# Early routing of tile 0, twice the early experts, and gate products in pairs in a transformer kernel

## The chip, the cores and the metric

The kernel runs on one core of one Trainium2 chip. The metric is device time in microseconds, measured over whole executions. Besides, one execution was recorded by the hardware profiler.

## The reference

Two transformer blocks over 512 tokens of width 1024. The first one mixes (attention, gated convolution) and then runs a layer of product-key experts, which is what the change touches. Cut to that:

```python
q = (hf @ w_query).reshape(t, 8, 256)
s1 = einsum('thd,hnd->thn', q[..., :128], peer_keys1)   # 128 scores
s2 = einsum('thd,hnd->thn', q[..., 128:], peer_keys2)
v1, i1 = top_k(s1, 16); v2, i2 = top_k(s2, 16)
cand = (v1[..., :, None] + v2[..., None, :]).reshape(t, 8, 256)
sc, ci = top_k(cand, 16)
idx = take(i1, ci // 16) * 128 + take(i2, ci % 16)      # 16 of 16384 experts, per head
gates = softmax(sc)
a = gelu(einsum('td,thkd->thk', hx, peer_u[idx]))
out = einsum('thk,thkd->td', gates * a, peer_v[idx])
```

The second block (MLA, HGRN2, feed-forward layers) follows and is not touched.

## The kernel before

Everything is float32 in effect: a matrix product is three TensorE passes (mm3) over a rounded high part and the rest. wload fetches 512 KB of weights (raw, four buffers), ScalarE rounds them to wh, VectorE subtracts to get wl (line 189; five buffers each). So each 512 KB costs one ScalarE and one VectorE pass before TensorE can use it.

Tokens form four tiles of 128. For tile 0 the experts are gathered: each of 256 steps (gathered, lines 754, 761, 770) has GpSimd fetch one 512 KB set of rows by an index tile (ui for peer_u, vi for peer_v; tile row, four buffers) and VectorE multiply it into a sum. The other three tiles (384 tokens) use all 16384 experts densely: 128 slices of peer_u give activations (expert_in, 24 matmuls into psu, Gelu to ga), which are multiplied by a dense gate matrix G, split into wgh and wgl, and multiplied with peer_v into the sums y.

The layer has two stages. *Routing* (peer_route): 16 query chunks on TensorE, whose scores VectorE ranks by top16 (five instructions for 16 values of one row set); topk ranks one head of one tile: two lists of 128 scores, then 80 candidate sums (cand), then those. Tiles 0 to 2 are ranked as the chunks come, tile 3 after tile 0 is finished (ui and vi written, line 702). For tiles 1 to 3 gate matrices follow, by one-hot masks (o, oh, ol; lines 729 to 732) and matmuls pg, stored to G. Into this stage are put *early experts*: fill keeps two running sums of assumed VectorE and TensorE time, and whenever TensorE's is behind, early runs expert_in for the next slice and stores its Gelu to DRAM (AD, line 800). There are 56 of these; two of their first subtractions run on GpSimd. *Products* (peer): 32 groups of four experts, first the 72 that were not early, then the 56 that were, whose ga are loaded from AD (seven buffers). Each ga is multiplied by its part of G (line 852) and split on its own. Gather steps are spread over the groups by a cost of 16 for a group of the first kind and 1 for one of the second.

```python
cost = [16 if e0 >= NE else 1.0 for e0 in groups]
rate = (256 - given[0]) / (sum(cost[:ng - 3]))
```

A scheduler decides each engine's final order by what waits for what; each engine then runs its list strictly in order.

Of the kernel before, what the change touches and what calls it, by code (L numbers as in the profile page):

```python
# [10 lines left out]
F32 = mybir.dt.float32  # L11
F16 = mybir.dt.float16
F32R = mybir.dt.float32r
I32 = mybir.dt.int32
U32 = mybir.dt.uint32
AF = mybir.ActivationFunctionType
ALU = mybir.AluOpType
# [140 lines left out]
class _Kernel:  # L158
# [421 lines left out]
        return out  # L580


    def expert_in(self, e2, pool=False):

        wh, wl = self.wload(self.a["peer_u"][e2], pool)
        ps = self.psa.tile([128, 512], F32, tag="a", name="psu")
        for k in range(8):
            s = slice(k * 128, k * 128 + 128)
            h, l = self.xs2[k]
            self.mm3(ps[:, :384], (wh[:, s], wl[:, s]), (h[:, 128:], l[:, 128:]), k == 0, k == 7)  # L590
        return ps[:, :384]
# [11 lines left out]
    def peer_route(self, p, G, fill, step):  # L603
# [14 lines left out]
        I = [p.tile([128, 4, 8, 16], U32, name=f"i{h}") for h in range(2)]  # L618
        SC = p.tile([128, 4, 8, 16], F32, name="SC")
        CI = p.tile([128, 4, 8, 16], U32, name="CI")  # L620
        qT, scores = {}, []

        def consume(n, ps):
            if n % 2 == 0:
                qT["k"] = p.tile([128, 2, 128], F32, tag="keys", name="keys", bufs=2)
                nc.sync.dma_start(qT["k"].rearrange("p a b -> p (a b)"), a["keys"][:, n * 128:(n + 2) * 128])
            o = self.work.tile([128, 512], F32, tag="full", name="qT", bufs=2)
            nc.scalar.activation(o, ps, AF.Copy)
            pt = self.pst.tile([128, 512], F32, tag="t", name="ptsc")
            for t in range(4):  # L630
                nc.tensor.matmul(pt[:, t * 128:(t + 1) * 128], o[:, t * 128:(t + 1) * 128], qT["k"][:, n % 2, :])
            if n % 8 == 0:
                scores.append(p.tile([128, 8, 4, 128], F32, tag="gt", name="sc", bufs=2))
            sc = scores[-1][:, n % 8]
            nc.scalar.activation(sc.rearrange("p a b -> p (a b)"), pt, AF.Copy)
            fill(1.2, 6.2)
            if n % 2 == 0:
                return
            for t in range(3):
                topk(t, n // 2)  # L640

        def topk(t, h):
            V = [self.small.tile([128, 16], F32, tag=f"v{x}", name=f"v{x}", bufs=2) for x in range(2)]
            for x in range(2):
                self.top16(V[x], I[x][:, t, h, :], scores[h // 4][:, h % 4 * 2 + x, t, :])


            cand = p.tile([128, 80], F32, tag="cand", name="cand", bufs=2)
            for i0, ni, nj, at in ((0, 2, 16, 0), (2, 2, 8, 32), (4, 4, 4, 48), (8, 8, 2, 64)):
                nc.vector.tensor_tensor(cand[:, at:at + ni * nj].rearrange("p (i j) -> p i j", j=nj),  # L650
                                        V[0][:, i0:i0 + ni, None].to_broadcast([128, ni, nj]),
                                        V[1][:, None, 0:nj].to_broadcast([128, ni, nj]), ALU.add)
            self.top16(SC[:, t, h, :], CI[:, t, h, :], cand)
            fill(3.0, 0.0)

        self.gemm_fm(self.xs2, [a["w_query"][c] for c in range(16)], consume)
        for t in range(4):
            sc = SC[:, t]
            g = p.tile([128, 8, 16], F32, tag="g", name="g", bufs=2)
# [18 lines left out]
            for x in range(2):  # L678
                ai = ij[x]
                af = p.tile([128, 8, 16], F16, tag="af", name="af", bufs=2)  # L680
                nc.vector.tensor_copy(af, ai)
                e = p.tile([128, 8, 16], F32, tag=f"e{x}", name=f"e{x}", bufs=2)
                for hh in range(2):

                    hs = slice(hh * 4, hh * 4 + 4)
                    ib = p.tile([128, 4, 16, 16], F16, tag="ib", name="ib", bufs=1)
                    nc.scalar.activation(ib, I[x][:, t, hs, :, None].to_broadcast([128, 4, 16, 16]), AF.Copy)
                    eq = p.tile([128, 4, 16, 16], F16, tag="eq", name="eq", bufs=1)
                    nc.vector.tensor_tensor(eq, iotaj[:, None].to_broadcast([128, 4, 16, 16]),
                                            af[:, hs, None, :].to_broadcast([128, 4, 16, 16]), ALU.is_equal)  # L690
                    nc.vector.tensor_tensor(eq, eq, ib, ALU.mult)
                    for w in (8, 4, 2):
                        nc.vector.tensor_tensor(eq[:, :, 0:w], eq[:, :, 0:w], eq[:, :, w:2 * w], ALU.add)
                    nc.vector.tensor_tensor(e[:, hs], eq[:, :, 0], eq[:, :, 1], ALU.add)
                    fill(2.2, 0.0)
                es.append(e.rearrange("p h k -> p (h k)"))
            fill(1.5, 0.3)
            if t == 0:
                ef = p.tile([128, 128], F32, tag="ef", name="ef", bufs=1)
                for dst, hi, lo in ((self.ui, es[0], es[1]), (self.vi, es[1], es[0])):  # L700
                    nc.vector.scalar_tensor_tensor(ef, hi, 128.0, lo, ALU.mult, ALU.add)
                    nc.vector.tensor_copy(dst, ef)
                nc.vector.tensor_copy(self.g0, g.rearrange("p h k -> p (h k)"))
                for tt in range(3, 4):
                    for h in range(8):
                        topk(tt, h)
                        for _ in range(2):
                            step()
                continue
            pt = self.pst.tile([128, 512], F32, tag="t", name="ptr")  # L710
            for n, src in enumerate((es[0], es[1], g.rearrange("p h k -> p (h k)"))):
# [8 lines left out]
            for c in range(4):  # L720
                gt = p.tile([128, 128, 32], F32, tag="gt", name="gt", bufs=2)
                for q in range(32 // BT):
# [10 lines left out]
                    for r0 in range(0, BT, 4):  # L733
                        pg = self.psv.tile([128, 4, 128], F32, tag="v", name="pg")
                        for r in range(4):
# [3 lines left out]
                        o = q * BT + r0  # L739
                        nc.scalar.activation(gt[:, :, o:o + 4].rearrange("p e t -> p t e"), pg, AF.Copy,  # L740
                                             scale=1.0 / 16384.0)
                    fill(2.5, 0.9)
                    step()
                nc.sync.dma_start(G[t * 4 - 4 + c], gt.rearrange("p e t -> p (e t)"))

# [27 lines left out]
    def peer(self):  # L773
        tc, nc, a = self.tc, self.nc, self.a
        NT = 384
        self.ui = self.keep.tile([128, 128], U32, name="ui")
        self.vi = self.keep.tile([128, 128], U32, name="vi")
        self.g0 = self.keep.tile([128, 128], F32, name="g0")
        with tc.tile_pool(name="peerd", bufs=1, space=DRAM) as pd, tc.tile_pool(name="p0", bufs=1) as p0:
# [9 lines left out]
            def step():  # L789
                if next(gat, self) is not self:  # L790
                    given[0] += 1

            with tc.tile_pool(name="p1", bufs=1) as p:
                spent = [0.0, 0.0]

                def early():
                    ga = p.tile([128, NT], F32, tag="ga", name="ga", bufs=4)
                    nc.scalar.activation(ga, self.expert_in(len(AD), not given[0]), AF.Gelu)  # L798
                    AD.append(pd.tile([128, NT], F32, name=f"AD{len(AD)}"))
                    nc.sync.dma_start(AD[-1], ga)  # L800
                    spent[0] += 0.0
                    spent[1] += 3.95

                def fill(vector, tensor):
                    spent[0] += vector
                    spent[1] += tensor
                    while spent[1] < spent[0] and len(AD) < 128:
                        early()

                def rstep():  # L810
                    step()
                    fill(1.15, 0.0)

                self.peer_route(p, G, fill, rstep)
                while len(AD) % 8:
                    early()
            NE = len(AD)
            self.psum(2, 1, 0)
            with tc.tile_pool(name="p2", bufs=1) as p:
# [1 line left out]
                groups = list(range(NE, 128, 4)) + list(range(0, NE, 4))  # L821
                ng = len(groups)

                cost = [16 if e0 >= NE else 1.0 for e0 in groups]
                rate = (256 - given[0]) / (sum(cost[:ng - 3]))
                due = [0.0]

                def spread(n):
                    due[0] += n
                    with tc.issue_after(mul.ins):  # L830
                        while due[0] >= 1.0:
                            step()
                            due[0] -= 1.0
# [4 lines left out]
                for gi, e0 in enumerate(groups):  # L838
# [3 lines left out]
                            nc.sync.dma_start(g[:, c].rearrange("p e t -> p (e t)"),  # L842
                                              G[c][:, e0 * 32:(e0 + 8) * 32])
                    ws = []
                    for e in range(4):
                        e2 = e0 + e
                        ga = p.tile([128, NT], F32, tag="ga", name="ga", bufs=7)
                        if e2 < NE:
                            nc.sync.dma_start(ga, AD[e2])
                        else:  # L850
                            nc.scalar.activation(ga, self.expert_in(e2), AF.Gelu)
                        mul = nc.vector.tensor_tensor(
                            ga.rearrange("p (c t) -> p c t", t=32), ga.rearrange("p (c t) -> p c t", t=32), g[:, :, gi % 2 * 4 + e, :], ALU.mult)
                        h = p.tile([128, NT], F32R, tag="wgh", name="wgh", bufs=8)
                        l = p.tile([128, NT], F32R, tag="wgl", name="wgl", bufs=8)
                        self.split(ga, h, l)
                        ws.append((h, l))
                        if e2 >= NE:
                            spread(rate * cost[gi] / 8)
                    if gi == 2:  # L860
                        gate2 = p.tile([128, 1024], F32, name="gate2")
                        gsteps = self.ada_row(5, "gate2", gate2, p)
# [503 lines left out]
```

## Time and profile before

| what | us |
|---|---|
| median of 3 runs (2957.12 to 2958.0) | 2957.59 |
| the profiled execution | 2946.67 |
| span of that execution, first to last instruction | 2944.9 |
| TensorE (PE) busy, share of the span | 2816.2, 96% |
| VectorE (DVE) busy | 1963.8, 67% |
| ScalarE (ACT) busy | 1132.1, 38% |
| GpSimd (POOL) busy | 332.7, 11% |

The queries begin near 268 us, the routing ends near 728, the products near 1562. The sum in the prediction is made against the profiled execution and then carried to the median.

### The profile page before, as it was taken

The numbers are of one execution on the slowest core, as the hardware profiler recorded it, in microseconds if no ns is written. First come the engines' busy times: TensorE is split into PE (matmuls) and PEld (weight loads), VectorE is DVE, ScalarE is ACT, GpSimd is POOL, SyncE is SP. The second block draws the span as 40 slices with busy tenths as digits, with TensorE's granted clock in tenths as the row PEclk, the third lists the DMA queues.
The fourth block names the chain that finished last, engine by engine and source line by source line (L and its number), as shares of the span: only waits on it lengthen the run. The fifth ranks groups of instructions, "written<-read, shape, count | busy, mean of one in ns | idle before, by whom it ended". The sixth has DMA issues, their size and how long they took to land.

```text
span 2944.9 us, 37577 instructions
## 1 busy us (share of the span) xinstructions
PE 2816.2 (96%) x14133; PEld 2382.1 (81%) x14133; DVE 1963.8 (67%) x3665; ACT 1132.1 (38%) x1672; POOL 332.7 (11%) x265
## 2 busy tenths in 40 slices
PE   6999959889999999999999999999999999999998
PEld 5777858788899999988787778888878887888887
DVE  8676999898778777886557666433474567634336
ACT  4454325566333333333346424222242233422223
POOL 0000023221334433440000000000000000000000
PEclk9999979899999999999999999999999999999999
DMA  8432368778999988899763103232321212323331
GB/s 294 149 105 86 101 199 301 284 295 315 361 320 323 323 313 307 312 325 308 229 188 119 57 29 115 89 118 94 100 91 63 86 58 65 115 86 112 102 95 51
DMA packets 182007, 521.34 MB, mean 177 GB/s; under 512 B 19776, under 2 KB 68544, under 8 KB 180288
## 3 DMA queue, kind: packets, MB, share of 16 engines
q1 hardware_dynamic: 144960, 384.70, 38.7%
q0 software_dynamic: 36864, 134.23, 12.8%
q8 instruction: 111, 1.82, 0.3%
q14 instruction: 72, 0.59, 0.1%
HBM read 478.48 MB, written 40.37 MB: 176 GB/s over the span
## 4 chain that ended last, share of the span: by engine, by line
PE 47%; DVE 2%; DMA 1%; ACT 0%; issue 0%; SPq 0%; DVEq 0%; ACTq 0%
PE psa L205 7%; PE psa L204 7%; PE psa L206 7%; PE psv L204 3%; PE psv L205 3%; PE psv L206 3%; PE psd L206 3%; PE psd L204 3%; PE psd L205 3%; PE pl L1274 1%; PE y L205 1%; PE y L206 1%; PE y L204 1%; PE pss L1013 1%; PE pt L289 1%; PE po L1030 1%
## 5 line engine op out<-in xcount | busy, mean ns | idle before, releaser
L186 ACT ACTIVATE wh<-raw 128x1024 fp32r<-128x1024 f32 x512 | 539.0, 1060 | 1199.3 <-PE psa L205 427.5
L189 DVE TENSOR_TENSOR wl<-raw,wh 128x1024 fp32r<-128x1024 f32 x510 | 620.3, 1222 | 338.4 <-ACT wh L186 323.9
L204 PE MATMUL psa<-xh,wh 128*128 128x512 f32 x1168 | 460.4, 397 | 4.3 <-ACT xh L300 2.8
L205 PE MATMUL psa<-xl,wh 128*128 128x512 f32 x1168 | 460.4, 395 | 1.9 <-DVE xl L307 1.9
L206 PE MATMUL psa<-xh,wl 128*128 128x512 f32 x1168 | 458.0, 393 | 0.5 <-DVE wl L189 0.5
L206 PE MATMUL psu<-xh,wl 128*128 128x384 f32 x1024 | 347.7, 340 | 22.3 <-DVE wl L189 22.3
L204 PE MATMUL psu<-xh,wh 128*128 128x384 f32 x1024 | 349.6, 341 | 16.0 <-ACT ga L798 11.6
L205 PE MATMUL psu<-xl,wh 128*128 128x384 f32 x1024 | 348.2, 340 | 0.0
L205 PE MATMUL y<-wl,wgh 128*128 128x512 f32 x768 | 299.6, 390 | 4.6 <-DVE wl L189 4.6
L206 PE MATMUL y<-wh,wgl 128*128 128x512 f32 x768 | 299.9, 391 | 0.0
L204 PE MATMUL y<-wh,wgh 128*128 128x512 f32 x768 | 298.9, 389 | 0.2 <-ACT wgh L186 0.2
L204 PEld LDWEIGHTS psa<-xh,wh 128*128 128x128 f32 x1168 | 220.8, 190 | 55.2 <-ACT xh L300 6.9
L205 PEld LDWEIGHTS psa<-xl,wh 128*128 128x128 f32 x1168 | 220.4, 189 | 48.1 <-DVE xl L307 3.6
L206 PEld LDWEIGHTS psa<-xh,wl 128*128 128x128 f32 x1168 | 220.4, 189 | 46.1 <-issue 1.0
L206 PEld LDWEIGHTS psu<-xh,wl 128*128 128x128 f32 x1024 | 194.8, 190 | 24.0 <-DVE wl L189 23.9
L204 PEld LDWEIGHTS psu<-xh,wh 128*128 128x128 f32 x1024 | 194.9, 190 | 23.1 <-ACT ga L798 13.9
L754 POOL DMA_INDIRECT row<-in_peer_u_rows,ui x128 | 162.2, 1267 | 426.1 <-DVE junk L761 242.0
L754 POOL DMA_INDIRECT row<-in_peer_v,vi x128 | 164.8, 1288 | 276.0 <-DVE y L770 256.4
L205 PEld LDWEIGHTS psu<-xl,wh 128*128 128x128 f32 x1024 | 194.8, 190 | 1.2 <-issue 0.5
L204 PE MATMUL psv<-wh,xh 128*128 128x512 f32 x464 | 185.4, 400 | 4.2 <-ACT xh L298 2.8
L205 PE MATMUL psv<-wl,xh 128*128 128x512 f32 x464 | 183.9, 396 | 0.0
L770 DVE SCALAR_TENSOR_TENSOR y<-row,au,y 128x1024 f32<-128x1024 f32 x127 | 162.8, 1282 | 30.8 <-DMA row<-in_peer_v,vi 30.2
(331 smaller groups left out, 4379.1 us busy)
## 6 DMA issues: line engine op xcount, KB each, us to landing
raw<-in_peer_u SPq DMA_DIRECT2D x128, 512.0 KB
raw<-in_peer_v SPq DMA_DIRECT2D x128, 512.0 KB
raw<-in_ffn_in SPq DMA_DIRECT2D x88, 512.0 KB
G<-gt SPq DMA_DIRECT2D x12, 2048.0 KB
g<-G SPq DMA_DIRECT2D x192, 128.0 KB
raw<-in_ffn_dn SPq DMA_DIRECT2D x44, 512.0 KB
rawa<-in_w_ada SPq DMA_DIRECT2D x64, 256.0 KB
AD<-ga SPq DMA_DIRECT2D x56, 192.0 KB
```

What stands on the lines that cost most here:

```text
L186: nc.scalar.activation(h, full, AF.Copy)
L189: (nc.gpsimd if pool else nc.vector).tensor_tensor(l, full, h.bitcast(F32), ALU.subtract)
L204: nc.tensor.matmul(out, A[0], B[0], start=first, stop=False)
L205: nc.tensor.matmul(out, A[0], B[1], start=False, stop=False)
L206: self.last_mm = nc.tensor.matmul(out, A[1], B[0], start=False, stop=last)
L289: nc.tensor.transpose(pt[:, (t - t0) * 128:(t - t0 + 1) * 128], xn[t][:, k * 128:(k + 1) * 128], self.ident)
L754: nc.gpsimd.indirect_dma_start(out=r, out_offset=None, in_=table, in_offset=bass.IndirectOffsetOnAxis(ap=idx[:, j:j + 1], axis=0))
L770: nc.vector.scalar_tensor_tensor(w, r, au[:, j:j + 1], w, ALU.mult, ALU.add)
L1013: nc.tensor.matmul(ps[:, :W], qr[h // 2][rb:rb + 64, q], kr[rb:rb + 64, :W], start=False, stop=True)
L1030: nc.tensor.matmul(po[:, q], v[j][:, h * 128:(h + 1) * 128], et[:, j * 128:(j + 1) * 128], start=j == 0, stop=j == i)
L1274: nc.tensor.matmul(pt[:P, o:o + 64], k[:, h, c * 128:c * 128 + P], qv[:, c, :, 1])
```

## The change

- Ranking is cut in two: best ranks the two lists of 128 of one head, sums builds the 80 candidate sums of all eight heads of a tile at once (four instructions of 128x8x16 and 128x8x32 instead of 32 small ones) and then ranks them head by head.
- While the query chunks run only tiles 0 and 1 get best. Right after them sums(0) and tile 0's indices follow; the sums of tile 1 and all of tiles 2 and 3 come behind tile 0, with a gather step after most pieces (40 in all instead of 16).
- The assumed times in fill change (vector time of wl is now counted, 1.2 per early expert; gather step 1.3; and others), and the number of early experts becomes 112.
- expert_load fetches an early expert's weights one ahead; the subtraction on GpSimd is gone.
- In the products ga, wgh and wgl hold two experts: one multiplication, one rounding and one subtraction for 768 columns.
- Gather steps: cost 13 for a group of four fresh experts, 4 for one of stored ones.

```diff
-    def expert_in(self, e2, pool=False):
-        wh, wl = self.wload(self.a["peer_u"][e2], pool)
+    def expert_load(self, e2):
+        if e2 < 128 and e2 not in self.uw:
+            self.uw[e2] = self.wload(self.a["peer_u"][e2])
+    def expert_in(self, e2):
+        self.expert_load(e2)
+        wh, wl = self.uw[e2]
...
-            fill(1.2, 6.2)
-            if n % 2 == 0:
-                return
-            for t in range(3):
-                topk(t, n // 2)
+            fill(1.2, 6.35)
+            if n % 2:
+                for t in range(2):
+                    best(t, n // 2)
+        def best(t, h):
+            if h == 0:
+                V[t] = [p.tile([128, 8, 16], F32, tag=f"v{x}", name=f"v{x}", bufs=2) for x in range(2)]
             for x in range(2):
-                self.top16(V[x], I[x][:, t, h, :], scores[h // 4][:, h % 4 * 2 + x, t, :])
+                self.top16(V[t][x][:, h], I[x][:, t, h, :], scores[h // 4][:, h % 4 * 2 + x, t, :])
+            fill(3.3, 0.0)
+        def sums(t, then):
+            cand = p.tile([128, 8, 80], F32, tag="cand", name="cand", bufs=1)
             for i0, ni, nj, at in ((0, 2, 16, 0), (2, 2, 8, 32), (4, 4, 4, 48), (8, 8, 2, 64)):
+                B = [128, 8, ni, nj]
+                nc.vector.tensor_tensor(cand[:, :, at:at + ni * nj].rearrange("p h (i j) -> p h i j", j=nj),
+                                        V[t][0][:, :, i0:i0 + ni, None].to_broadcast(B),
+                                        V[t][1][:, :, None, 0:nj].to_broadcast(B), ALU.add)
+            fill(1.3, 0.0)
+            for h in range(8):
+                self.top16(SC[:, t, h, :], CI[:, t, h, :], cand[:, h])
+                fill(1.4, 0.0)
+                then()
         self.gemm_fm(self.xs2, [a["w_query"][c] for c in range(16)], consume)
+        sums(0, lambda: None)
...
-                    fill(2.2, 0.0)
+                    fill(3.4, 0.0)
...
-                for tt in range(3, 4):
+                sums(1, step)
+                for tt in range(2, 4):
                     for h in range(8):
-                        topk(tt, h)
-                        for _ in range(2):
-                            step()
+                        best(tt, h)
+                        step()
+                    sums(tt, step)
...
-                    fill(2.5, 0.9)
+                    fill(2.8, 1.0)
...
-                    nc.scalar.activation(ga, self.expert_in(len(AD), not given[0]), AF.Gelu)
+                    self.expert_load(len(AD))
+                    self.expert_load(len(AD) + 1)
+                    nc.scalar.activation(ga, self.expert_in(len(AD)), AF.Gelu)
-                    spent[0] += 0.0
-                    spent[1] += 3.95
+                    spent[0] += 1.2
+                    spent[1] += 4.2
...
-                    fill(1.15, 0.0)
+                    fill(1.3, 0.0)
...
-                cost = [16 if e0 >= NE else 1.0 for e0 in groups]
+                cost = [13 if e0 >= NE else 4.0 for e0 in groups]
...
+                    for e in range(0, 4, 2):
+                        ga = p.tile([128, 2, NT], F32, tag="ga", name="ga", bufs=4)
+                        for i in range(2):
+                            e2 = e0 + e + i
+                            if e2 < NE:
+                                nc.sync.dma_start(ga[:, i], AD[e2])
+                            else:
+                                nc.scalar.activation(ga[:, i], self.expert_in(e2), AF.Gelu)
+                        mul = nc.vector.tensor_tensor(g4, g4, g[:, :, q:q + 2, :].rearrange("p c e t -> p e c t"), ALU.mult)
+                        h = p.tile([128, 2, NT], F32R, tag="wgh", name="wgh", bufs=4)
+                        l = p.tile([128, 2, NT], F32R, tag="wgl", name="wgl", bufs=4)
+                        self.split(ga, h, l)
```

Two places in VectorE's list. The first: the finish of tile 0. Before, from the cast that writes vi it is 47 rows to the next wl of an early expert, and six gather products (junk) come first; the last rows of these are (v, i: ranking of scores; cand, CI: candidate sums):

```order
L761 SCALAR_TENSOR_TENSOR junk,au<-row,h_98 128x1024
L599 MAX_INDEX CI<-SC,cand 128x8
L598 MAX v_3624<-sc 128x8
L598 MAX v_3625<-sc 128x8
L599 MAX_INDEX i_2123<-v_3624,sc 128x8
L599 MAX_INDEX i_2124<-v_3625,sc 128x8
L650 TENSOR_TENSOR cand<-v_3624,v_3625 128x16 x2
L601 MATCH_REPLACE sc<-v_3625,sc 128x128
L650 TENSOR_TENSOR cand<-v_3624,v_3625 128x16
L189 TENSOR_TENSOR wl<-raw,wh 128x1024
```

Now, the same place, from the cast on:

```order
L717 CAST vi<-ef 128x128
L603 MAX SC<-cand 128x8 x2
L604 MAX_INDEX CI<-SC,cand 128x8 x2
L189 TENSOR_TENSOR wl<-raw,wh 128x1024
L606 MATCH_REPLACE cand<-SC,cand 128x80
L603 MAX SC<-cand 128x8 x2
L604 MAX_INDEX CI<-SC,cand 128x8 x2
L606 MATCH_REPLACE cand<-SC,cand 128x80
L603 MAX SC<-cand 128x8 x2
L604 MAX_INDEX CI<-SC,cand 128x8
L777 SCALAR_TENSOR_TENSOR junk,au<-row,h_98 128x1024
```

The wl has moved ahead of the first gather product, to the third row behind the cast.

The second: VectorE's list in the products, among experts whose ga come from AD (ga: product with g; wgl: split; wl: weights of peer_v; y_2113: gather product of tile 0). Before:

```order
L852 TENSOR_TENSOR ga<-ga,g 128x384
L189 TENSOR_TENSOR wgl<-ga,wgh 128x384
L189 TENSOR_TENSOR wl<-raw,wh 128x1024
L852 TENSOR_TENSOR ga<-ga,g 128x384
L770 SCALAR_TENSOR_TENSOR y_2113<-row,au,y_2113 128x1024
L189 TENSOR_TENSOR wgl<-ga,wgh 128x384
L189 TENSOR_TENSOR wl<-raw,wh 128x1024
```

Now, one group of four:

```order
L875 TENSOR_TENSOR ga<-ga,g 128x768
L189 TENSOR_TENSOR wgl<-ga,wgh 128x768
L189 TENSOR_TENSOR wl<-raw,wh 128x1024
L875 TENSOR_TENSOR ga<-ga,g 128x768
L189 TENSOR_TENSOR wl<-raw,wh 128x1024
L786 SCALAR_TENSOR_TENSOR y_2113<-row,au,y_2113 128x1024 x2
L189 TENSOR_TENSOR wgl<-ga,wgh 128x768
L189 TENSOR_TENSOR wl<-raw,wh 128x1024
L786 SCALAR_TENSOR_TENSOR y_2113<-row,au,y_2113 128x1024 x2
L189 TENSOR_TENSOR wl<-raw,wh 128x1024
L786 SCALAR_TENSOR_TENSOR y_2113<-row,au,y_2113 128x1024
```

Product and split come half as often and twice as wide, and four to five gather products stand in each group where there was one in some four.

## Rows read from the trace of the kernel before

**Rows 1.** The page's first line.
```profile
span 2944.9 us, 37577 instructions
```
**Rows 2.** Windows: busy time of PE, PEld, DVE, ACT, POOL; clock, DMA share, GB/s.
```profile
400.00:450.00 50.00, 35.87 (x177) 34.60 (x178) 48.29 (x202) 11.88 (x16) 16.86 (x15) 0.80 0.82 275
...
350.00:750.00 400.00, 335.52 (x2274) 310.56 (x2273) 361.54 (x946) 213.93 (x252) 85.62 (x69) 0.93 0.74 268
740.00:1310.00 570.00, 568.82 (x2890) 518.81 (x2889) 449.65 (x537) 208.29 (x278) 228.41 (x177) 1.00 0.92 322
```
**Rows 3.** Waits of TensorE, 350 to 750: total us, times, longest.
```profile
PE psu L206 <- DVE wl L189: 22.3, 4, 20.8
PE psu L204 <- ACT ga L798: 11.6, 7, 4.3
PE ptr L712 <- DVE e L694: 11.0, 6, 4.0
PE pg L737 <- ACT gt L740: 6.9, 14, 1.1
PE pg L738 <- DVE ol L732: 5.7, 10, 0.7
```
**Rows 4.** Timeline of TensorE, 690 us: start, duration.
```profile
690.13 0.33 PE L205 MATMUL psu<-xl,wh 128*128 128x384 f32 x1
690.30 0.34 PE L206 MATMUL psu<-xh,wl 128*128 128x384 f32 x1
...
690.55 0.22 PE L737 MATMUL pg<-oh,o 128*128 128x128 f16 x1
690.61 0.22 PE L738 MATMUL pg<-ol,o 128*128 128x128 f16 x1
```
**Rows 5.** Timeline of VectorE, 600 us.
```profile
600.10 1.22 DVE L189 TENSOR_TENSOR wl<-raw,wh 128x1024 fp32r<-128x1024 f32 x1
601.23 0.69 DVE L731 TENSOR_TENSOR oh<-ol,eT 128x1024 f16<-128x1024 f16 x1
```
**Rows 6.** Timeline of VectorE, 338 us, in the ranking.
```profile
338.75 0.07 DVE L601 MATCH_VALUE_LOAD cand<-SC,cand 128x8 f32 x1
...
338.95 0.08 DVE L599 MATCH_VALUE_LOAD i<-v,sc 128x8 f32 x1
...
339.22 0.23 DVE L598 MAX8 SC<-cand 128x8 f32<-128x80 f32 x1
339.36 0.28 DVE L598 MAX8 v<-sc 128x8 f32<-128x128 f32 x1
```
**Rows 7.** Gathers: tile row (first and last start), and its group by line, 230 to 780.
```profile
L754 POOL DMA_INDIRECT row<-in_peer_u_rows,ui x128: 932/1077/1975, 391.4 to 928.3; - x128
L761 DVE SCALAR_TENSOR_TENSOR junk<-row,h x128: 1198/1219/1272, 395.9 to 942.9; 128x1024 f16<-128x1024 f32 x128
...
L761 DVE SCALAR_TENSOR_TENSOR junk<-row,h 128x1024 f16<-128x1024 f32 x76 | 92.7, 1220 | 9.3 <-DMA row<-in_peer_u_rows,ui 9.3
```
**Rows 8.** Windows as in rows 2, with dense transfers, and one of stored experts.
```profile
440.00:490.00 50.00, 46.92 (x271) 46.15 (x271) 45.56 (x98) 23.28 (x30) 21.11 (x15) 1.00 0.92 334
750.00:800.00 50.00, 49.96 (x245) 44.27 (x244) 41.35 (x64) 16.97 (x22) 24.13 (x19) 1.00 1.01 384
1350.00:1400.00 50.00, 50.00 (x222) 41.42 (x221) 27.49 (x40) 18.83 (x26) 3.63 (x2) 1.00 0.88 287
```
**Rows 9.** Timeline of VectorE, 1395 to 1445, stored experts.
```profile
1399.63 0.56 DVE L852 TENSOR_TENSOR ga<-ga,g 128x384 f32<-128x384 f32 x1 [3.06 <-DMA ga<-AD]
...
1408.37 0.55 DVE L189 TENSOR_TENSOR wgl<-ga,wgh 128x384 fp32r<-128x384 f32 x1
...
1435.29 0.56 DVE L852 TENSOR_TENSOR ga<-ga,g 128x384 f32<-128x384 f32 x1 [3.52 <-DMA ga<-AD]
...
1442.13 0.56 DVE L852 TENSOR_TENSOR ga<-ga,g 128x384 f32<-128x384 f32 x1 [1.26 <-DMA ga<-AD]
```
**Rows 10.** Timeline of SyncE's queue, same stretch: an issue of an AD load.
```profile
1430.65 0.32 SPq L849 DMA_DIRECT2D ga<-AD  x1
```

More of the change, by code (lines that the diff above doesn't have):

```diff
@@ L620, in peer_route @@
         CI = p.tile([128, 4, 8, 16], U32, name="CI")
-        qT, scores = {}, []
+        qT, scores, V = {}, [], {}
         def consume(n, ps):
@@ L635, in consume @@
             nc.scalar.activation(sc.rearrange("p a b -> p (a b)"), pt, AF.Copy)
-            fill(1.2, 6.2)
-            if n % 2 == 0:
-                return
-            for t in range(3):
-                topk(t, n // 2)
-        def topk(t, h):
-            V = [self.small.tile([128, 16], F32, tag=f"v{x}", name=f"v{x}", bufs=2) for x in range(2)]
+            fill(1.2, 6.35)
[5 more added lines that the diff above has]
+                V[t] = [p.tile([128, 8, 16], F32, tag=f"v{x}", name=f"v{x}", bufs=2) for x in range(2)]
             for x in range(2):
-                self.top16(V[x], I[x][:, t, h, :], scores[h // 4][:, h % 4 * 2 + x, t, :])
-            cand = p.tile([128, 80], F32, tag="cand", name="cand", bufs=2)
+                self.top16(V[t][x][:, h], I[x][:, t, h, :], scores[h // 4][:, h % 4 * 2 + x, t, :])
+            fill(3.3, 0.0)
+        def sums(t, then):
+            cand = p.tile([128, 8, 80], F32, tag="cand", name="cand", bufs=1)
             for i0, ni, nj, at in ((0, 2, 16, 0), (2, 2, 8, 32), (4, 4, 4, 48), (8, 8, 2, 64)):
[L650 to L654, printed above, removed]
+                B = [128, 8, ni, nj]
[7 more added lines that the diff above has]
+                then()
         self.gemm_fm(self.xs2, [a["w_query"][c] for c in range(16)], consume)
+        sums(0, lambda: None)
         for t in range(4):
@@ L775, in peer @@
         NT = 384
+        self.uw = {}
         self.ui = self.keep.tile([128, 128], U32, name="ui")
@@ L844, in peer @@
                     ws = []
[L845 to L855, printed above, removed]
+                    for e in range(0, 4, 2):
[6 more added lines that the diff above has]
+                                nc.scalar.activation(ga[:, i], self.expert_in(e2), AF.Gelu)
+                        q = gi % 2 * 4 + e
+                        g4 = ga.rearrange("p e (c t) -> p e c t", t=32)
+                        mul = nc.vector.tensor_tensor(g4, g4, g[:, :, q:q + 2, :].rearrange("p c e t -> p e c t"), ALU.mult)
+                        h = p.tile([128, 2, NT], F32R, tag="wgh", name="wgh", bufs=4)
+                        l = p.tile([128, 2, NT], F32R, tag="wgl", name="wgl", bufs=4)
                         self.split(ga, h, l)
-                        ws.append((h, l))
-                        if e2 >= NE:
-                            spread(rate * cost[gi] / 8)
+                        ws += [(h[:, i], l[:, i]) for i in range(2)]
+                        if e0 >= NE:
+                            spread(rate * cost[gi] / 4)
                     if gi == 2:
```

## The prediction

> **What bounds the kernel now.** First the totals: the profiled execution took 2946.67 us, of which the span is 2944.9 [rows 1]; the runs shown have a median of 2957.59, 10.9 more, so my sum is a difference, subtracted from either. A difference within 0.2% (5.9 us) can't be told from none. Then the windows by stage, where TensorE's busy time falls short of the window: in the routing, 350 to 750 us, it was busy 335.5 of 400 [rows 2], in the products that follow almost always (568.8 of 570, the same rows). So only the routing has something to give: 64.5 us idle. About 5 of it lie after 730 at the change of pools, which the change leaves: 59.5. The granted clock averaged 0.93 there, and 0.80 from 400 to 450 [rows 2]. If the slow share fell on busy time it cost up to 0.07 x 335.5 = 23 us, if on idle time nothing; I take 10. **Recoverable: 70 us.**
>
> The waits of TensorE [rows 3] say for whom: mostly early experts' matmuls (psu) for wl, once 20.8 us, and for the Gelu that frees a bank, then transposes for VectorE. VectorE was busy 361.5 of the 400 us. It bounds the routing, and an in-order queue puts ranking ahead of wl.
>
> **The price of an expert.** psu matmuls start 0.173 us apart [rows 4]: 24 make 4.15 us. y matmuls run 222 in the 50 us from 1350 [rows 8]: 18 make 4.05. The mask matmuls (pg) start 0.06 apart [rows 4]. VectorE starts its next operation about 0.08 before the last ends: wl holds it 1.13 [rows 5], a gather product (1.22, [rows 7]) also 1.14. In the ranking [rows 6] a 128-wide MAX8 reads 0.28 and so holds 0.20, a find with its load 0.27 (the replace alike); on 80 candidates the three take 0.14, 0.21 (estimate) and 0.20.
>
> **Part by part.**
> (1) *56 early experts become 112* (counted stores of AD). 56 x 4.15 = 232 us of TensorE leave the products and enter the routing: in sum nothing, but they fill the 59.5 idle us if VectorE keeps up. Their wl move too (56 x 1.14 = 64 us), and 88 gather steps instead of 64 lie in the routing, 168 instead of 192 behind.
>
> (2) *Ranking two tiles, sums of eight heads at once.* 128 small sums (0.09 each, estimate from the 0.14 on 80) become 16 of 128 and 256 elements (0.2 to 0.34, estimate): 11 us become 4, on VectorE alone. In the 16 query chunks VectorE now has some 78 us of work against 93 of TensorE; before it had 116 up to the index tiles.
>
> (3) *Finish of tile 0.* Here a wait stays. In the new order 67 candidate operations (12.4 us), 42 of index arithmetic (11.5), four sums and wl make 25.4 us between the sixth and seventh wl. Five wl buffers cover 5 x 4.15 = 20.8; 4.6 stay as a stall. Shortly after, seven gather products stand between two wl: 11.3 us against 4.15, with nothing in hand: 7.1. Sum 12. The first gather took 4.5 us from issue to use [rows 7], and later ones come at 2.6 us when transfers are dense (19 in 50 us, [rows 8]) where the product takes 1.14; by that the burst of eight costs up to 10, part of it under ranking: I take 6 (0 to 10). Before, the same place cost 39.2 us from one wl to the next.
>
> (4) *Ranking of tiles 2 and 3 beside experts.* From the 10th to the 56th expert VectorE has 46 wl (52.4), 60 gather products (68.4) and 63.8 of the rest, 184.6 us, or 4.01 per expert against 4.15. It is 97% full. Gathers in the routing were waited for 9.3 us up to 780 [rows 7], at most 0.15 for each of the 64 steps of the routing: 4.01 + 1.3 x 0.15 = 4.2, so about 2 us; with twice the wait 11. I take 6 (0 to 24, the end at 0.5 each).
>
> (5) *Masks.* From the 57th expert VectorE has 227.8 us for 55 experts that hold TensorE 228 and, with 768 mask matmuls at 0.06 between, 274: TensorE bounds. The waits of pg (6.9 + 5.7, [rows 3]) fell where no expert stood between; I take 2 (0 to 14). The clock: what is left of the stalls is a third of before, so 3 of the 10.
> Routing: 12 + 6 + 6 + 2 + 3 = 29 left of 70, **41 gained** (58 if only the 12 stay; about 11 with all upper ends).
>
> (6) *Weights one ahead.* The order keeps seven to nine loads ahead of the store of AD, before six at times and then ten. No term of its own, it is what lets (1) run; two wl leave GpSimd. Covered by TensorE; without that cover 2 x 1.14.
>
> (7) *Products in pairs.* 128 products and 128 splits of 384 become 64 of 768. By 0.47 for 384 (0.55 less 0.08, [rows 9]) and 1.14 for 1024 a pair holds (estimate) VectorE 0.87: 9 us less, off the path. What matters is a loop: a product waits for its AD load, which waits for the split that frees the buffer. Before, ten products in a row came at 4.25 us each against 4.05 of TensorE, each waiting for its load; issue to use up to 4.6 us there [rows 9, 10]. That stretch lived on earlier slack. With 100 experts of this kind the slack would not do; in pairs the loop is 0.87 + 0.87 + 0.6 + 0.4 + 4.6 = 7.3 (0.6 from split to issue and 0.4 for the second issue, estimates) against 8.1. VectorE has 13.4 to 13.9 us per group of four against 16.2, plus one short lead per group (1.14 of work where the load takes up to 4.6): I take 6 us for all groups (0 to 20).
>
> (8) *Steps 13 to 4.* 168 steps spread over 4 groups with fresh experts (14.4 each) and 25 with stored ones (4.4 each). TensorE: 16 x 8.2 + 100 x 4.05 = 536 us. Bytes: u 8.4, v 60.8, AD 19.7, G 22.8, gathers 88.1, w_ada 8.4 = 208 MB, 388 GB/s. The nearest row: 384 GB/s over 50 us with TensorE busy 49.96 [rows 8]. At 384 it takes 542: 6 us over. The far end: 322 at a DMA share of 0.92 (740 to 1310, [rows 2]) is 350 at 1, 595 us, 59 over. I take 6, the row with the same kinds of traffic side by side.
> The Trainium skill (DMA: Bandwidth & Descriptors, Specifications) gives about 358 GB/s from HBM as a core's limit; its section on bandwidth has 425 measured on a single core in transfers of 16 MB. Estimates from that page: by the first (8) would be 46 over, and the change a loss of some 11 us; by the second nothing over. This trace, of one core with transfers of 512 KB and less, stands between: 384 over 50 us [rows 8].
>
> **Sum:** 41 - 6 - 6 = 29. The profiled execution would be 2917.7, the median **2928.6 us**.
>
> **Rivals.**
> *Transfers bound the products (slower).* Mechanism of (8): below 361 GB/s (208 MB in 536 + 41) the products lose more than the routing gains. At 350: 41 - 6 - 59 = -24, 2981. For it: more than a fifth of the bytes are rows of 1 and 1.5 KB (G, AD), and gathers block VectorE in order. Against it: the 384. Chance 0.20. The Trainium skill's 358 GB/s (DMA: Bandwidth & Descriptors, Specifications) is this rival at the edge, by estimate some 2969; no row here shows such a limit.
> *Ranking bounds the routing.* Gather waits of 0.5 us each: (4) costs 24, 29 - 18 = 11 gained, 2946.6. For it: 71 gathers in about 215 us beside 50 loads of experts, some 340 GB/s, when the like stretch, 440 to 490, kept TensorE busy only 46.9 of 50 [rows 8]. Against: 0.15 per gather so far. Chance 0.14.
> *Everything is hidden.* Only the 12 of (3) and nothing in the products: 58, 2899.6. Chance 0.12.
> That the experts don't move is excluded by the order (112 stores).
> *The forecast,* between 2912 and 2943: chance 0.54.
>
> **Numbers.** The range takes in the forecast, the second and third cases and the better half of the first: 2898 to 2968. Faster by over 5.9 us (below 2951.7): 0.54 x 0.97 + 0.14 x 0.7 + 0.12 + 0.20 x 0.1 = 0.76; same 0.09; slower 0.15.
>
> **What would show it.** Right: TensorE's idle time between 350 and the change of pools near 900 is 20 to 35 us, most of it near 390 to 420; psu waits for wl fall from 22 to about 18; the products, near 920 to 1540, run at 370 to 390 GB/s with TensorE busy over 97%. Wrong: between 350 and 930 it is idle over 45 us; or TensorE waits for wl or wgl all through the products while ScalarE waits for raw and VectorE for rows (first rival); or psu waits for wl evenly from 420 to 600 (second).

## The result and the profile after

The change is slower: 2995.66 us (four runs, 2994.06 to 3001.28) against 2957.36 (four runs, 2952.46 to 2958.0), a ratio of 1.0142, 95% interval 1.0125 to 1.0158. I had forecast 2928.6, with 2968 as the upper end. The profiled executions differ by 47.4 us of span, 2992.3 against 2944.9 [rows 1], the medians by 38.3: the profiled execution before was a quick one of its kind.

The matmuls y cut both kernels at the same point. Here the group of the last pass, before and after, with first and last start:

```profile
L206 PE MATMUL y<-wh,wgl x768: 388/389/796, 749.3 to 1562.2; 128*128 128x512 f32 x192
```
```profile
L206 PE MATMUL y<-wh,wgl x768: 387/389/796, 941.3 to 1607.7; 128*128 128x512 f32 x192
```

56 more experts stand ahead of the first y, 56 x 4.15 = 232.4 us. So the products should begin at 749.3 + 232.4 = 981.7 if nothing else changed; they begin at 941.3. **The routing gained 40.4 us; forecast 41.** From first to last y it took 812.9 - 232.4 = 580.5 us for the same work before, now 666.4. **The products lost 85.9 us; forecast 12.** The whole miss lies there. Windows of the change, with the columns of [rows 2]:

```profile
350.00:450.00 100.00, 82.50 (x437) 79.40 (x436) 88.39 (x393) 34.15 (x44) 26.15 (x19) 0.90 0.62 208
450.00:550.00 100.00, 99.90 (x577) 99.58 (x576) 99.78 (x372) 36.81 (x50) 34.77 (x29) 1.00 0.93 307
550.00:650.00 100.00, 83.52 (x513) 81.13 (x512) 88.60 (x160) 44.74 (x57) 38.43 (x30) 0.90 0.88 316
...
1050.00:1150.00 100.00, 80.10 (x317) 63.41 (x316) 75.39 (x71) 25.09 (x27) 44.71 (x30) 0.90 0.93 339
1250.00:1350.00 100.00, 85.82 (x352) 67.51 (x351) 78.45 (x74) 30.67 (x32) 42.88 (x28) 0.95 0.93 335
1350.00:1450.00 100.00, 87.53 (x358) 69.40 (x357) 64.48 (x60) 27.71 (x29) 31.57 (x21) 0.92 0.83 287
1450.00:1550.00 100.00, 90.21 (x368) 72.78 (x367) 65.83 (x63) 31.50 (x35) 21.32 (x14) 0.92 0.79 274
941.30:1607.70 666.40, 604.94 (x2591) 495.33 (x2590) 494.58 (x507) 202.52 (x225) 253.38 (x164) 0.95 0.88 316
```

In the routing TensorE idles in two places only (17.5 and 16.5 us), and VectorE is full between them. In the products it idles 61.5 us (666.4 - 604.94), while VectorE is busy 74% and the DMA share is 0.79 to 0.93: no engine and no queue is full where TensorE waits. Waits of VectorE, then of TensorE, 1240 to 1570 (total, times, longest):

```profile
DVE ga L875 <- DMA ga<-AD: 97.5, 26, 8.0
...
DVE y L786 <- DMA row<-in_peer_v,vi: 1.6, 1, 1.6
...
PE y L205 <- DVE wl L189: 35.9, 13, 5.7
```

VectorE stands 97.5 us at products whose AD load has not landed, and TensorE waits for wl, which is queued behind. VectorE's timeline over two such waits:

```profile
1414.95 0.96 DVE L875 TENSOR_TENSOR ga<-ga,g 128x768 f32<-128x768 f32 x1 [1.54 <-DMA ga<-AD]
1415.82 0.95 DVE L189 TENSOR_TENSOR wgl<-ga,wgh 128x768 fp32r<-128x768 f32 x1
1416.69 1.22 DVE L189 TENSOR_TENSOR wl<-raw,wh 128x1024 fp32r<-128x1024 f32 x1
1424.73 0.96 DVE L875 TENSOR_TENSOR ga<-ga,g 128x768 f32<-128x768 f32 x1 [6.82 <-DMA ga<-AD]
1425.61 1.22 DVE L189 TENSOR_TENSOR wl<-raw,wh 128x1024 fp32r<-128x1024 f32 x1
1426.74 2.60 DVE L786 SCALAR_TENSOR_TENSOR y<-row,au,y 128x1024 f32<-128x1024 f32 x2
1429.26 0.95 DVE L189 TENSOR_TENSOR wgl<-ga,wgh 128x768 fp32r<-128x768 f32 x1
...
1436.16 0.95 DVE L875 TENSOR_TENSOR ga<-ga,g 128x768 f32<-128x768 f32 x1
1437.03 0.95 DVE L189 TENSOR_TENSOR wgl<-ga,wgh 128x768 fp32r<-128x768 f32 x1
1437.89 1.22 DVE L189 TENSOR_TENSOR wl<-raw,wh 128x1024 fp32r<-128x1024 f32 x1
1445.40 0.96 DVE L875 TENSOR_TENSOR ga<-ga,g 128x768 f32<-128x768 f32 x1 [6.29 <-DMA ga<-AD]
```

SyncE's queue, issues of the loads of those pairs, and all loads of AD from 1250 to 1540 with the median time from issue to landing:

```profile
1416.88 1.90 SPq L870 DMA_DIRECT2D ga<-AD  x2
...
1430.24 0.80 SPq L870 DMA_DIRECT2D ga<-AD  x2
...
1438.00 1.08 SPq L870 DMA_DIRECT2D ga<-AD  x2
```
```profile
ga<-AD SPq DMA_DIRECT2D x58, 192.0 KB, 5.8
```

The split that ends at 1416.77 frees a buffer, the loads issue at 1416.88, and the next product in VectorE's list is already the one that uses them: it starts at 1424.73. The same at 1438.00 and 1445.40. One group of two pairs takes 20.7 us (1424.73 to 1445.40) where TensorE needs 16.2; over 1250 to 1550 a pair takes 10.0 us in the mean (1078 matmuls, 36 to a pair). There are four pair buffers, but the list has each product right behind the split that frees its own buffer, or a few rows behind it, so in this stretch only one pair's loads are on their way at a time.

### The profile page after: what moved, and what is told of

Read it like the earlier page. It is cut to its first block, busy times and chain, and to the rows that moved or that the text cites. A ratio compares the mean times of both kernels' runs of the same rounds, so it can differ in the third digit from the quotient of the medians.

```text
span 2992.3 us, 37544 instructions
## 1 busy us (share of the span) xinstructions
PE 2834.0 (95%) x14133; PEld 2393.3 (80%) x14133; DVE 1952.8 (65%) x3427; ACT 1116.1 (37%) x1608; POOL 375.8 (13%) x263
## 4 chain that ended last, share of the span: by engine, by line
PE 58%; DMA 15%; issue 12%; DVE 12%; ACT 2%; POOL 1%; SPq 0%; DVEq 0%; POOLq 0%; ACTq 0%
PE psa L204 9%; PE psa L205 9%; PE psa L206 9%; DMA row<-in_peer_u_rows,ui 4%; PE psv L204 4%; PE psv L205 4%; PE psv L206 4%; DMA ga<-AD 3%; DVE wl L189 3%; PE psd L206 3%; PE psd L204 3%; PE psd L205 3%; DMA g<-G 3%; DMA row<-in_peer_v,vi 2%; DVE junk L777 2%
## 5 line engine op out<-in xcount | busy, mean ns | idle before, releaser
L205 PE MATMUL y<-wl,wgh 128*128 128x512 f32 x768 | 311.7, 406 | 48.4 <-DVE wl L189 47.8
L206 PE MATMUL psu<-xh,wl 128*128 128x384 f32 x1024 | 346.4, 339 | 11.3 <-DVE wl L189 11.3
L204 PE MATMUL y<-wh,wgh 128*128 128x512 f32 x768 | 307.2, 401 | 11.4 <-ACT wgh L186 11.4
L206 PE MATMUL y<-wh,wgl 128*128 128x512 f32 x768 | 308.2, 402 | 1.2 <-DVE wgl L189 1.2
L770 POOL DMA_INDIRECT row<-in_peer_u_rows,ui x128 | 170.3, 1330 | 590.1 <-DVE junk L777 387.1
L770 POOL DMA_INDIRECT row<-in_peer_v,vi x128 | 204.6, 1598 | 280.8 <-DVE y L786 262.2
L205 PEld LDWEIGHTS y<-wl,wgh 128*128 128x128 f32 x768 | 150.1, 195 | 89.8 <-DVE wl L189 58.3
L204 PEld LDWEIGHTS y<-wh,wgh 128*128 128x128 f32 x768 | 148.9, 194 | 46.2 <-ACT wgh L186 13.7
```

The costliest lines, as they stand in the source:

```text
L204: nc.tensor.matmul(out, A[0], B[0], start=first, stop=False)
L205: nc.tensor.matmul(out, A[0], B[1], start=False, stop=False)
L206: self.last_mm = nc.tensor.matmul(out, A[1], B[0], start=False, stop=last)
L770: nc.gpsimd.indirect_dma_start(out=r, out_offset=None, in_=table, in_offset=bass.IndirectOffsetOnAxis(ap=idx[:, j:j + 1], axis=0))
```

## The experiments

Experts are called stored where their ga come back from AD, and fresh where they are computed in the products. Theories: **A**, this standing of VectorE in its order; **B**, transfers too slow for the products; **C**, the round trip of 112 experts through AD costs what it gains; **D**, the pairs.

**First batch.** e1_delay adds one order edge for stored pairs and nothing else. By the code it puts a product behind the second wl of the same pair two groups earlier, that is of the pair four before it, whose split frees its buffer; the text of the expectation says two.

```diff
+ at = len(wls) - 8 + e + 2
+ with (tc.issue_after(wls[at - 1].ins) if e0 < NE and at > 0 else ExitStack()):
      mul = nc.vector.tensor_tensor(g4, g4, ...)
...
  vs.append(self.wload(a["peer_v"][e0 + e]))
+ wls.append(self.sub)
```

> The change, with one order edge more: in a group of stored experts the product of a pair is queued on VectorE behind the weights' subtraction of a pair two earlier, so that it comes about 16 us later in VectorE's list and its AD load has that long to land. Loads, buffers and bytes are the same. Theory A (VectorE stands still at a product until its own AD load has landed, 97.5 us of waits from 1240 to 1570, and the weights of peer_v stand behind it): the waits of VectorE for AD fall below 25 us, TensorE's waits for wl in that stretch from 36 us to under 10, the clock there from 0.91 back to 0.97 or more; time 2945 to 2960. Theory B (the transfers themselves are too slow for the products): nothing changes, 2985 to 3000. Theory C (too many stored experts, whatever the order): 2985 to 3000 as well.

Measured: 2938.48 us, ratio 0.9947 (0.9928 to 0.9966). The windows of this kernel, and VectorE's waits for AD, 1240 to 1570:

```profile
1050.00:1150.00 100.00, 78.43 (x310) 62.04 (x309) 74.30 (x70) 23.66 (x26) 43.90 (x30) 0.90 0.92 335
1250.00:1350.00 100.00, 99.54 (x438) 81.79 (x437) 92.06 (x86) 37.09 (x39) 51.74 (x31) 1.00 1.04 395
1350.00:1450.00 100.00, 100.00 (x443) 82.84 (x442) 89.64 (x83) 37.80 (x40) 50.85 (x31) 1.00 1.04 394
943.00:1554.30 611.30, 584.51 (x2591) 487.04 (x2590) 495.29 (x507) 203.26 (x225) 263.17 (x164) 0.98 0.93 345
```
```profile
DVE ga L878 <- DMA ga<-AD: 10.0, 7, 3.9
```

Theory A holds: the same loads, bytes and buffers, the waits down from 97.5 to 10.0, and the products 55 us shorter, 34.7 of it idle time of TensorE and 20.4 shorter matmuls. The time lies below A's range. B and C fall: among stored experts TensorE is busy almost throughout at 394 to 395 GB/s, more than in any window of the change above. What is left is 26.8 us idle, nearly all before 1150, which the edge did not touch.

e2_nogather takes the rows of the products' steps from a tile that is there (`return self.h2` in row).

> The change, without the gather transfers in the products stage: each of its steps multiplies a tile that is already in the chip's memory in place of the gathered rows, so VectorE's work stays and 88 MB and GpSimd's work go (the output leaves out the experts of tile 0 that were gathered there). Theory A: AD loads land in about 3 us in place of 5.9, so VectorE's waits for AD fall from 97 to some 30 to 50 us but stay, and TensorE's idle time from 940 to 1600 falls from 61 to under 15: 2925 to 2945. Theory B: no waits of VectorE for AD over 10 us in sum, TensorE idle under 8: 2920 to 2930. Theory C (the round trip through AD itself): idle stays over 30 us, 2960 to 2985.

Measured: 2900.06 us, ratio 0.9820 (0.9798 to 0.9843), faster than any theory had it.

```profile
941.40:1515.10 573.70, 573.02 (x2591) 481.98 (x2590) 491.69 (x507) 204.05 (x225) 0.00 (x0) 1.00 0.68 214
```
```profile
DVE ga L879 <- DMA ga<-AD: 41.4, 15, 5.2
```

VectorE still stands 41.4 us at products (1240 to 1515), as A said, but TensorE loses 0.7 us: without the gathers' traffic, which lengthens it, the standing does no harm. The row also gives the price of the products' matmuls at full clock, 573.0 us.

e3_single puts the former loop of one expert at a time back (seven ga buffers, 128 products of 384).

> The change with the products written as before: one expert at a time, 128 products and splits of 384, seven buffers for ga, eight for the halves. Theory A: a chain of load, product and split per expert instead of per pair, 5.9 us of landing against 4.05 of TensorE, so VectorE waits for AD more than the 97 us of the change and the time is 3005 to 3040. Theory D (the pairs are what went wrong, since a wait now holds two experts): 2950 to 2970. Theories B and C: 2990 to 3005, as the change.

Measured: 2990.36 us, ratio 1.0123 (1.0098 to 1.0149), as the change. VectorE stood 98.8 us in 41 waits: more of them and shorter, not more in sum, so A's price for singles was too high. D falls.

e4_cap56 stops early experts at 56 (`and len(AD) < 56`).

> The change with its early experts stopped at 56, the number of before. Theory A: from 1240 on there are 7 stored groups less and the gathers lie with fresh experts, so the waits for AD fall to a half or less, the clock is at 0.97 or more in the products, and the early experts' gain in the routing is given back: TensorE idle 50 to 70 us there; 2950 to 2970. Theory B: bytes are nearly the same (10 MB less of AD), the products still starve: 2980 to 3000. Theory C: as before or better, 2935 to 2957.

Measured: 3034.62 us, ratio 1.0279 (1.0255 to 1.0303), outside all three. The cap lets the first 56 be spent by 650 us, so TensorE has no filler during the masks (126.7 busy of the 200 us from 650). The first y comes at 822.5, 73 us later than before, while the products take 824.6 against 812.9. So the run tested where the early experts lie more than how many there are; e7 mends that.

**Second batch.** What is left before 1150, and the cover. e5_delay_even is e1 with

```diff
-cost = [13 if e0 >= NE else 4.0 for e0 in groups]
-rate = (256 - given[0]) / (sum(cost[:ng - 3]))
+cost = [9 if e0 >= NE else 5.0 for e0 in groups]
+rate = (256 - given[0]) / (sum(cost[:ng - 2]))
```

> The change with the order edge of the first experiment (2938.5 us), and its gather steps spread more evenly: cost 9 and 5 in place of 13 and 4, over one group more, so some 9 steps in a group of fresh experts (14.4 before) and 5 in a stored one (4.4). Theory A2 (what is left in the products, 26 us of TensorE idle from 950 to 1150, comes from the crowd of gathers in the fresh groups, where a gather lands after 8 us): the idle time there falls to under 10 and nothing new appears later; 2912 to 2927. Theory S (it comes from the switch to stored experts, where SyncE issues up to a dozen loads of AD and two dozen of G ahead of the weights): 20 us or more stay idle; 2930 to 2945. Theory B (5 gathers per stored group are too many bytes): TensorE falls idle all through 1150 to 1500, 2945 or more.

Measured: 2920.19 us, ratio 0.9873 (0.9850 to 0.9897).

```profile
950.00:1150.00 200.00, 192.72 (x907) 166.74 (x906) 156.60 (x182) 66.28 (x76) 87.56 (x58) 0.98 0.97 357
1150.00:1450.00 300.00, 293.74 (x1275) 240.71 (x1274) 272.08 (x253) 102.45 (x108) 156.56 (x99) 0.99 1.04 393
939.50:1532.90 593.40, 579.85 (x2592) 484.74 (x2590) 493.79 (x507) 203.92 (x225) 256.01 (x164) 0.99 0.95 355
```

Idle before 1150 fell from 26 to 7.3 us, as A2 said, so the spread of the steps decides what is lost there, and the switch alone (S) does not. But the switch is in both kernels. SyncE's queue in the change, its weights of peer_v around the switch:

```profile
1050.48 0.33 SPq L195 DMA_DIRECT2D raw<-in_peer_v  x1
...
1074.28 6.09 SPq L195 DMA_DIRECT2D raw<-in_peer_v  x4
```

Between them it issues loads of AD, G and w_ada, and ScalarE then waits 17.4 us for weights. In e5 no weights are issued from 1037.0 to 1055.8 either, and ScalarE waits 17.1 us, but TensorE loses little by it. How the crowd of gathers takes away the reserve for this wait was not taken apart. 6.3 us came back later, at 393 GB/s and a share of 1.04; no run holds more than 396 over 100 us, so this is probably the limit of the transfers.

e6_before_delay: the same edge in the kernel before.

> The kernel before with the same order edge on its stored products (one expert each). There VectorE also waited for AD, 58.9 us in 32 waits, but TensorE lost 4.6 us by it. Theory A says that the wait costs only where VectorE has no room behind it (57% busy there, 65 to 80% in the change): 0 to 5 us faster, 2945 to 2953. If the edge is worth over 15 us here too, the wait was the loss in both kernels, and the change's own cost is something else.

Measured: 2950.0 us, ratio 0.9976 (0.9961 to 0.9990): some 7 us, against 57 in the change. VectorE's waits for AD fell from 58.9 to 11.6 us there too, but TensorE had been idle only 4.7 us in all of the products: the edge pays where VectorE is short of room.

e7_delay_thin is e1 with 56 early experts spread over the whole routing (`spent[1] += 8.0`).

> The change with the order edge, and with 56 early experts spread evenly over the routing (8.0 in place of 4.2 us of assumed TensorE time each) in place of 112. Theory A: the early experts were worth their place in the routing: TensorE's idle time from 350 to the end of the routing rises from 33 to 60 us or more, the products lose little; 2950 to 2975. Theory C (the AD round trip of 112 experts costs what it gains): 2925 to 2940.

Measured: 3023.84 us, ratio 1.0225 (1.0203 to 1.0247).

```profile
268.00:350.00 82.00, 82.00 (x414) 67.43 (x413) 49.78 (x226) 32.12 (x47) 0.24 (x1) 1.00 0.31 97
350.00:850.00 500.00, 390.19 (x2385) 358.28 (x2384) 431.72 (x1194) 220.11 (x259) 117.66 (x99) 0.86 0.71 256
```

The window of the query chunks in the kernel before:

```profile
268.00:350.00 82.00, 82.00 (x414) 67.80 (x413) 79.75 (x519) 30.89 (x44) 4.82 (x3) 1.00 0.30 97
```

110 us idle in the routing, which ends 79 us later than before (first y at 828.1 against 749.3). The products take 807.8 us here; those of e5, which spreads its steps otherwise, take 593.4 + 232.4 = 825.8 for the same work, so the 56 more round trips cost some 18 us with all their traffic, less than half of the 40 that the routing gained. C falls for good. The new routing needs the 112: beside the query chunks VectorE now does 49.8 us of work where it did 79.75, and 24 more gather steps of 1.14 follow; by that estimate 57 us more lie where VectorE bounds. My 2950 to 2975 had left that out. The remaining 22 us and the clock of 0.86 weren't taken apart.

e8_delay_single: edge and singles.

> The change with the order edge and with the products one expert at a time (as in the third experiment). Theory A: the edge heals singles as it heals pairs, and the pairs are worth VectorE time that nobody waits for: 2935 to 2948, within 10 us of the first experiment. If pairs matter: 2955 or more.

Measured: 2932.97 us, ratio 0.9911 (0.9890 to 0.9933), a little under A's range. The edge heals singles too, and pairs gain nothing.

**Third batch.** e9_even has the even steps without the edge; e10_even_single the edge, the even steps and singles.

> The change with the even gather steps of the fifth experiment (9 and 5, one group more) and without the order edge. Theory A: five gathers in every stored group and VectorE still standing at each product: the waits for AD from 1150 on are 100 us or more and TensorE's idle time there 35 us or more; only the part before 1150 is healed; 2970 to 2995. If the even spread alone were enough (Theory A2 for all of the loss): 2920 to 2940.

Measured: 2976.74 us, ratio 1.0059 (1.0040 to 1.0078). From 950 to 1150 TensorE idles 10.2 us (25.0 in the change), from 1250 to 1550 43.9:

```profile
950.00:1150.00 200.00, 189.76 (x885) 163.86 (x885) 153.30 (x180) 64.03 (x74) 84.70 (x57) 0.97 0.95 350
1250.00:1550.00 300.00, 256.06 (x1012) 202.20 (x1011) 209.88 (x194) 86.29 (x92) 101.89 (x70) 0.91 0.86 306
```

The waits for AD were 82 us, not the 100 that I had put, the rest as A said.

> Order edge, even gather steps, and products one expert at a time: the two repairs together on singles. By the earlier runs singles with the edge stood at or a little under pairs, so 2910 to 2925, within 8 us of the fifth experiment; if the pairs were of use once the gathers lie evenly: 2930 or more.

Measured: 2920.74 us, ratio 0.9877 (0.9861 to 0.9893), the same as with pairs.

| ratio to before | no edge | edge |
|---|---|---|
| steps 13 and 4 | 1.0142 | 0.9947 |
| steps 9 and 5 | 1.0059 | 0.9873 |

The edge is worth 1.9 to 2.0%, the even steps 0.7 to 0.8%, each with or without the other. So the two causes are separate, and with both repaired (e5) the kernel beats the one before by 1.27% (1.03 to 1.50).

## Why the prediction was wrong

**Right in sum, in part by luck: parts (1) to (5).** The routing gained 40.4 us for 41 forecast. Part (3) put 12 + 6 near 390 to 420; 17.5 us idle there. Parts (4) and (5) put 6 + 2 behind it, with ends of 24 and 14; 16.5 were measured near 600 and 1.4 behind, a single pg wait of 11.6 us for a mask among them, where gathers, some waiting for their rows, and weights stand ahead of the mask in VectorE's list. In sum TensorE idled 35.5 us from 350 to 950, where 26 were put and 5 more left at the change of pools. Up to the first y its idle time fell from 64.5 to 35.4, by 29.0 where 33.5 had been forecast; the rest came from matmuls: busy 334.8 us before and 555.9 - 232.4 = 323.5 now, 11.3 less at a granted clock of 0.97 instead of 0.93, where I had taken 7 (10 less 3). Two errors cancelled. (With all upper ends the working leaves 70 - 63 = 7, not about 11.) These are the waits of TensorE, 350 to 900, that answer to [rows 3]:

```profile
PE pg L753 <- DVE oh L747: 11.6, 1, 11.6
PE psu L206 <- DVE wl L189: 11.3, 2, 8.6
PE psu L204 <- ACT ga L818: 11.1, 4, 4.2
```

**Wrong: part (7), 6 us (0 to 20) for the loop of AD.** By e1 it was about 57 us. The loop was seen, but mis-sized at 7.3 us per pair against 8.1 of TensorE; measured 10.3 in the group shown, 10.0 in the mean. Two terms failed. The landing: I took the 4.6 of the kernel before; here the median is 5.8, behind 0.8 to 1.9 of issue, and a product started 7.4 to 7.9 us after its first issue. And the loop was taken to hold the product and the split only, while up to 3.7 us of weights and gather products stand between the two (1425.61 to 1429.26), because the same change puts four to five gathers in each group. My upper bound was the slack of a group, not the length of this loop with its new neighbours. And slower matmuls behind the stalls, 20 of the 55 us in the products, were put at nothing.

**Wrong: part (8), 6 us (0 to 59), as to its place.** I priced the steps by bytes over all the products. As bytes the price was good: e5, with another spread and the edge, idles 6.3 us in its dense part, at 393 GB/s where I took 384. What failed was the spread: 14.4 steps in a fresh group, ahead of the switch to stored experts, cost about 20 us (e9, e5) that no term held; how they do it stays open in part. The 85.9 us lost in the products split up into 55.1 for the edge (666.4 to 611.3), 17.9 for the even steps (to 593.4) and 12.9 that e5 still loses.

**The rivals.** Transfers bound the products was the rival on the slower side, and most of its sign came true, its mechanism did not. From 1240 to 1570 TensorE waited for wl (35.9 us) and ScalarE for raw (196.1), as it said, but VectorE waited 1.6 us for rows and 97.5 for AD, which it did not say. The change draws 274 to 339 GB/s while TensorE waits, less than e1 does without waiting. The Trainium skill (DMA: Bandwidth & Descriptors, Specifications) puts a core's limit from HBM at about 358 GB/s; the runs don't agree for a core alone, with 394 to 395 GB/s over 200 us of e1. The rival that would have held is one I did not write down: VectorE standing at an AD load that is issued one split before, with wl behind it. The working of (7) had its product, split and load, but not what stands between them.

## What to carry to other kernels

Buffers give lead only if the consumer is also late in its engine's list: look where in the in-order queue the operation that waits for a load stands against the one that lets the load be issued. When more work moves onto that engine, price the loop again with everything that will then stand inside it, and with the landing times of the new traffic. Spread bulk transfers by where the waiting engine has room, and not by bytes alone.

## What the runs showed of the hardware

Idle time of TensorE cost about half as much again in slower matmuls. The products' matmuls take 573.0 us at a granted clock of 1.00 (e2), 604.9 in the change, which idles 61.5 us at a mean clock of 0.95: 32 us more. In e1 26.8 idle came with 11.5 more, in e5 13.6 with 6.8, in e9 54.2 with 31.4. Part of them ran at the lower of the two levels, 1.2 GHz instead of 2.4: in the change TensorE stood for 4.5 us until 1426.88, the y matmuls then started 0.43 us apart until 1431.3, at a granted clock of 0.50 from 1426 to 1430, and 0.23 apart behind that, at 1.00 from 1432. The idle windows show clocks of 0.90 to 0.95; I had priced the stalls of the products without this.
